# A two-block transformer layer on one core: the lo half of every fourth half unit of weights comes from an accumulating GpSimd DMA onto the negated hi half

## The chip, the cores and the metric

The kernel runs on one core of one Trainium2 chip. The core has a matrix engine (TensorE, PE in the profile; its weight loads are PEld), VectorE (DVE), ScalarE (ACT), GpSimd (POOL) and SyncE (SP), which issues most DMAs, and 16 DMA engines that all queues share. The metric is the device time of one execution in microseconds; lower is better.

## The reference

256 tokens of width 2048 pass through two blocks in fp32. Block 1 is differential attention beside retention, cross attention to a memory of 256 tokens, and a gated feed-forward; block 2 is spatial gating beside a gated linear recurrence, and a convolved feed-forward. Nearly all arithmetic lies in products of 256 rows with large weight matrices, for example:

```python
    h = rmsnorm(x, norm_mix_g[l])
    proj = h @ w_in[l]                     # 2048 x 6144
    ...
    x = x + mixed @ w_o[l]                 # 2048 x 2048
    ...
    x = x + (jax.nn.silu(hf @ w_gate[l]) * (hf @ w_up[l])) @ w_down[l]   # 2048 x 5632, 5632 x 2048
```

The results must hold to fp32-like accuracy.

## The kernel before

TensorE's fast format is fp32r, which keeps fewer bits than fp32. The kernel therefore splits each operand into two fp32r parts: `hi`, the value rounded, and `lo`, the value minus `hi`. A product is made of three matmuls, hi by hi, hi by lo and lo by hi.

The weights are a fixed list (`seq`) of 452 units of 1 MB, [128, 2048] fp32 each, in the order of their use. Every unit is used once. `fetch` loads a unit by one DMA on SP's queue into one of three raw buffers (tile `w`). `push` takes half a unit, 128x1024, and splits it: ScalarE casts it into `hi` (tile `wh`, line 129) and VectorE writes `lo` as the raw half minus `hi` (tile `wl`, line 130). `wh` and `wl` have five buffers each. The last five half units are split into other tiles, so 899 half units go through `wh` and `wl`.

`half` hands one half unit to a GEMM. Before it does, it pushes until five half units are in the list, so a half unit is split four half units ahead of its use. With five buffers, the buffers of half unit k are those of half unit k-5: the cast of half unit k starts when TensorE is done with half unit k-5, and is followed by the use of k-4, k-3, k-2 and k-1 before TensorE comes to k.

There are two kinds of GEMM. `gemm_fm` makes 256 output features by 256 tokens; a half unit is 8 matmuls with `wh` on 512 columns (line 297: the tokens' hi and lo side by side) and 8 with `wl` on 256 columns (line 301). Its first `wl` matmul is the second matmul of the half unit. There are 84 such GEMMs of four half units each. `gemm_tm` makes 256 tokens by 512 output features; a half unit is 12 matmuls on 512 columns (`mm3`, lines 145 to 147), and the first that reads `wl` (line 146) is again the second one.

Small work between the GEMMs (softmax, norms, convolutions, the scan) runs as generators that `tick` steps once per half unit. Each engine takes its instructions in its own order. GpSimd's queue holds 21 reciprocal square roots (`rsqrt`, line 151), 14 additions of squares (line 413) and two masks; it issues no DMA.

Of the kernel before, what the change touches and what calls it, by code (L numbers as in the profile page):

```python
# [8 lines left out]
F32 = mybir.dt.float32  # L9
F32R = mybir.dt.float32r  # L10
# [12 lines left out]
LOOKAHEAD = 4  # L23
TAIL = 5  # half units at the end whose operands stay for a second pass

# columns of the packed per-feature vectors
_COLS = [
# [17 lines left out]
def tile_kernel(ctx, tc, x, xT, mem, memT, par, alibi, rdecay, ident_d, bc_rows, gm_wsT,  # L45
# [29 lines left out]
    class Pair:  # L75
        """two k-tiles of a split operand: tiles of (hi | lo), or a tile of hi and one of lo"""

# [13 lines left out]
        def fill(self, src, gcols=None):  # L91
            """hi + lo == src * gain; src [P, 2, S] or two of [P, S]"""
            if gcols is None and not self.joined:
                split(self.t[0], self.t[1], src)
            else:
                for k in range(2):
                    split(self.hi(k), self.lo(k), src[:, k, :], None if gcols is None else gcols[k])
            return self
# [6 lines left out]

# [1 line left out]
    pr = cpool.tile([P, NPAR], F32, name="pr")  # L107
# [6 lines left out]
    V.memset(mhalf, -0.5)  # L114
    # the first activation table loads while the first data comes
    A.activation(st(1), mhalf[:, 0:1], AF.Square)
# [8 lines left out]

# [1 line left out]
    def split(hi, lo, src, gcol=None):  # L127
# [7 lines left out]
    def xpose_split(src, c, gcols=None, joined=False):  # L135
        """token-major src[t][:, c:c+256] -> split feature-major pair"""
        pt = sps().rearrange("p (k s) -> p k s", k=2)
        for k in range(2):
            for t in range(2):
                T.transpose(pt[:, k, t * P:(t + 1) * P], src[t][:, c + k * P:c + (k + 1) * P], ident)  # L140
        return Pair(joined).fill(pt, gcols)

    def mm3(out, lh, rh, start, stop):
        """both operands as (hi, lo)"""
        T.matmul(out, lhsT=lh[0], rhs=rh[0], start=start, stop=False)  # L145
        T.matmul(out, lhsT=lh[0], rhs=rh[1], start=False, stop=False)  # L146
        T.matmul(out, lhsT=lh[1], rhs=rh[0], start=False, stop=stop)  # L147
# [6 lines left out]
    class Sq:  # L154
        """sums of squares of token-major rows, piece by piece"""

# [18 lines left out]
    def rows(c):  # L175
        """[P tokens, 2] columns -> [P, 256], the same row in every partition"""
        d = flat(ft())[:, 0:S]
        for t in range(2):
            V.tensor_scalar(d[:, t * P:(t + 1) * P], ident, c[:, t:t + 1], None, ALU.mult)
        ps = sps()  # L180
        T.matmul(ps[:, 0:S], lhsT=ones, rhs=d, start=True, stop=True)
        r = spool.tile([P, S], F32, tag="rows", name=nm("rows"), bufs=3)
        A.copy(r, ps[:, 0:S])
        return r
# [3 lines left out]

# [1 line left out]
    seq = [(w_in_f, 0, u) for u in range(2)]  # L190
# [37 lines left out]
    def push():  # L228
        """one more half unit on its way"""
        w, g, u = seq[pos[1] // 2]  # L230
        h = pos[1] % 2
        if not raws:
            fetch()
        r = raws[0][:, 1024 * h:1024 * h + 1024]
        if h == 1:
            raws.pop(0)
        pos[1] += 1
        if pos[1] > 2 * len(seq) - TAIL:
            # kept until both halves of the tokens have used them
            hi, lo = [flat(rt()) for _ in range(2)], [flat(rt()) for _ in range(2)]  # L240
            for k in range(2):
                split(hi[k], lo[k], r[:, 512 * k:512 * k + 512])
        else:
            hi = whi.tile([P, 1024], F32R, tag="h", name=nm("wh"))
            lo = wlo.tile([P, 1024], F32R, tag="l", name=nm("wl"))
            split(hi, lo, r)
        feed.append((w, g, u, h, hi, lo))
# [10 lines left out]

# [1 line left out]
    bg = []  # L260
# [21 lines left out]
    def gemm_fm(wap, g, acts):  # L282
        """256 output features x 256 tokens: [P, m, (hi parts | lo parts)]"""
        ps = psg.tile([P, 2, 512], F32, tag="g", name=nm("pg"))
# [27 lines left out]
    def gemm_tm(wap, g, acts, k0=0, ps=None, tail=0):  # L312
        """256 tokens (2 banks) x 512 output features; in the last `tail` half units the second
        half of the tokens waits for the function that is returned"""
        if ps is None:
# [39 lines left out]
    def evac_split(ps, c):  # L355
        """token-major, as (hi, lo) for each half of the tokens"""
        res = []
        for t in range(2):
            hi, lo = flat(rt()), flat(rt())
            split(hi, lo, ps[t], need(c, 0)[:, t:t + 1])  # L360
            res.append((hi, lo))
        return res
# [10 lines left out]
    def operands(g, acts, gcols):  # L373
        """columns 512 g of the residual as operands of a GEMM"""
        for p in range(2):
# [4 lines left out]
    def next_in(g, acts, sq, gcols, after=None):  # L380
        """behind a residual update of columns 512 g"""
        if acts is not None:
# [8 lines left out]
    def stats(sq, rc, rr=None):  # L391
        """rstd of the rows as columns, and as a row in every partition"""
        rc[0] = sq.rstd(D)
# [4 lines left out]

    # =================================================================
    # block 1: projections, differential attention, retention  # L400
    # =================================================================
    def load(src, p):
# [4 lines left out]
    def load_split(f, gname, p, sq):  # L407
        a = Pair(True).fill(f, [col(gname, 2 * p + j) for j in range(2)])
        # sum of squares, feature-major
        s = ft()  # L410
# [7 lines left out]
    def col_stats(sq, n):  # L418
        """feature-major squares -> rstd as columns"""
        tot = sps()  # L420
# [10 lines left out]
    def x_gen():  # L431
        # loads (L), weight units (W) and splits (S) in the order in which they start
        n = 0
# [26 lines left out]

    # lambda = exp(q1.k1) - exp(q2.k2) + lam_init
    lam_init = 0.8 - 0.6 * math.exp(-0.3 * 0)
# [17 lines left out]
    def av_stage(pT, v, off):  # L480
        """[q, 256] = P^T.T @ v, causal in blocks of 128, and its sums of squares"""
        po = sps().rearrange("p (t e) -> p t e", t=2)
# [123 lines left out]

    # memory
    hm_a, sqm = [None] * 8, []
# [29 lines left out]

    # =================================================================
    # cross attention  # L640
    # =================================================================
    xk = []
# [6 lines left out]
    for g in range(4):  # L649
        if g == 3:  # L650
            # takes the space of the memory's operands, pair by pair
            spawn(chain([operands(i, hx_a, cols("norm_x_g", 0, 16)) for i in range(4)]))
# [50 lines left out]

    # =================================================================
    # feed-forward 1
    # =================================================================
    gg = cpool.tile([P, 16], F32, name="gg")
# [9 lines left out]
    def second_norm(g):  # L717
        # block 2 takes rmsnorm(x) * norm_f_g and normalises it again
        gf = flat(ft())
# [20 lines left out]

    # =================================================================
    # block 2: spatial gating and recurrent branch
    # =================================================================
    def tok(ins):
        # one order for the functions that share no activation table
        tc.stamp_issue_order_token(ins.ins, "tables")
        return ins
# [18 lines left out]

    # softplus(-lam) = max(-lam, 0) + log1p(exp(-|lam|))
    c8 = cpool.tile([P, 2, 8], F32, name="c8")
# [26 lines left out]
    def v_norm(t):  # L795
# [13 lines left out]
        for g in range(2):  # L809
            V.scalar_tensor_tensor(vg[t][g], vg[t][g], rr, gvg[g], ALU.mult, ALU.mult)  # L810
            V.tensor_tensor(vg[t][g], vg[t][g], gvb[g], ALU.add)
            yield
        # mixing over tokens, token-major
        for g in range(2):
# [10 lines left out]
    for f in ws:  # L825
        # keep s <= t
        f3 = f.rearrange("p (h t) -> p h t", t=P)
# [20 lines left out]

# [1 line left out]
    wa, wx = big(lru_wa), big(lru_wx)  # L850
# [29 lines left out]
    def lru_scan():  # L880
        for p in range(4):
# [5 lines left out]
            yield  # L887
            # 1 - exp(-2z) = tanh(z) * (1 + exp(-z)^2)
            d_ = ft()
# [84 lines left out]

    # =================================================================
    # feed-forward 2
    # =================================================================
    def conv3(z, c0):
# [36 lines left out]

    # last columns: the first half of the tokens leaves while the second is computed
    ps = [sps(), sps()]
# [98 lines left out]
```

## Time and profile before

| | |
|---|---|
| time, median of 2 runs | 2611.34 us (2611.17 to 2611.5) |
| span of the profiled execution | 2611.1 us |
| PE, PEld busy | 2590.6 us (99%), 2192.4 us (84%) |
| DVE, ACT, POOL busy | 1575.4 us (60%), 1292.5 us (50%), 38.1 us (1%) |
| HBM read | 486.39 MB, 187 GB/s over the span |
| granted TensorE clock | 0.999 of full speed |

The span runs from the first to the last instruction. The two timed runs lie 0.1 and 0.4 us above it, so next to nothing lies around the span. Matmuls overlap, so that a matmul of 390 ns is followed by the next after some 227 ns; the start times, not the durations, tell TensorE's pace.

### The profile page before, as it was taken

How to read it: one execution, taken by the hardware profiler on the slowest of the kernel's cores; microseconds unless marked ns; L12 is line 12 of the kernel's file. 1: busy time of each engine (PE TensorE's matmuls, PEld its weight loads, DVE VectorE, ACT ScalarE, POOL GpSimd, SP SyncE). 2: the span in 40 equal slices, each digit the busy share in tenths (PEclk: the TensorE clock that was granted, in tenths of full speed). 3: DMA queues.
4: the chain of work that ended last, by engine and by line, in shares of the span. 5: the costliest groups of instructions: out<-in, count | busy, mean ns of one | idle time of the engine just before them, and what ended most of it. 6: DMA issues, size and time to landing. Idle time of an engine off the chain costs nothing.

```text
span 2611.1 us, 32123 instructions
## 1 busy us (share of the span) xinstructions
PE 2590.6 (99%) x12922; PEld 2192.4 (84%) x12922; DVE 1575.4 (60%) x1889; ACT 1292.5 (50%) x1683; POOL 38.1 (1%) x41
## 2 busy tenths in 40 slices
PE   8999999999999999999999999999999999999998
PEld 7888888888888888888888888888888888888887
DVE  6665565556555454545454557866777745777754
ACT  5555554454454444334444555755555534555543
POOL 1000010000000000000000000000000000000000
PEclk9999999999999999999999999999999999999999
DMA  6455555554455555555555555554555555555563
GB/s 245 172 177 202 200 203 185 187 184 157 158 177 186 188 191 193 191 193 187 188 192 193 199 200 190 178 193 177 192 181 188 185 193 190 194 182 189 180 215 137
DMA packets 72726, 490.57 MB, mean 188 GB/s; under 512 B 8193, under 2 KB 8321, under 8 KB 14593
## 3 DMA queue, kind: packets, MB, share of 16 engines
q1 hardware_dynamic: 72576, 488.52, 53.2%
q8 instruction: 101, 1.65, 0.2%
q14 instruction: 49, 0.39, 0.0%
HBM read 486.39 MB, written 2.10 MB: 187 GB/s over the span
## 4 chain that ended last, share of the span: by engine, by line
PE 98%; issue 0%; DVE 0%; ACT 0%; DMA 0%; POOL 0%; SPq 0%; ACTq 0%; POOLq 0%; DVEq 0%
PE pg L297 24%; PE pg L145 19%; PE pg L146 19%; PE pg L147 19%; PE pg L301 12%; PE pp L140 1%; PE pp L147 1%; PE pp L146 1%; PE pp L145 1%; DMA w<-in_w_in_f_dram 0%; DVE r L133 0%; PE pp L818 0%; PE pp L871 0%; PE pp L870 0%; ACT junk L163 0%
## 5 line engine op out<-in xcount | busy, mean ns | idle before, releaser
L130 DVE TENSOR_TENSOR wl<-w,wh 128x1024 fp32r<-128x1024 f32 x899 | 1101.4, 1226 | 840.9 <-ACT wh L129 836.1
L129 ACT CAST wh<-w 128x1024 fp32r<-128x1024 f32 x899 | 944.1, 1051 | 983.2 <-PE pg L147 737.6
L297 PE MATMUL pg<-r,wh 128*128 128x512 f32 x2688 | 945.8, 401 | 12.0 <-ACT wh L129 7.3
L145 PE MATMUL pg<-wh,r 128*128 128x512 f32 x2224 | 870.2, 391 | 0.0
L147 PE MATMUL pg<-wh,r 128*128 128x512 f32 x2224 | 867.9, 390 | 0.0
L146 PE MATMUL pg<-wl,r 128*128 128x512 f32 x2224 | 867.5, 390 | 0.0
L301 PE MATMUL pg<-r,wl 128*128 128x256 f32 x2688 | 731.3, 283 | 0.5 <-DVE wl L130 0.5
L297 PEld LDWEIGHTS pg<-r,wh 128*128 128x128 f32 x2688 | 497.1, 189 | 120.0 <-ACT wh L129 7.3
L301 PEld LDWEIGHTS pg<-r,wl 128*128 128x128 f32 x2688 | 510.6, 190 | 17.6 <-DVE wl L130 1.0
L147 PEld LDWEIGHTS pg<-wh,r 128*128 128x128 f32 x2224 | 417.8, 188 | 86.4
L146 PEld LDWEIGHTS pg<-wl,r 128*128 128x128 f32 x2224 | 418.0, 188 | 85.6 <-DVE wl L130 0.4
L145 PEld LDWEIGHTS pg<-wh,r 128*128 128x128 f32 x2224 | 417.8, 188 | 84.4
L343 DVE TENSOR_TENSOR f<-pg,f 128x512 f32<-128x512 f32 x84 | 58.0, 691 | 90.2 <-ACT f L342 90.2
L342 ACT COPY f<-pg 128x512 f32<-128x512 f32 x84 | 49.2, 586 | 125.4 <-PE pg L297 125.4
L985 DVE SCALAR_TENSOR_TENSOR f<-f,pr,f 128x255 f32<-128x255 f32 x192 | 79.9, 478 | 0.7 <-ACT f L982 0.7
L982 ACT ACTIVATE f<-f,pr 128x256 f32<-128x256 f32 x96 | 52.6, 595 | 26.2 <-DVE f L344 26.1
L344 DVE TENSOR_TENSOR f<-f,rows 128x512 f32<-128x512 f32 x84 | 58.1, 691 | 2.6
L129 ACT CAST r<-f 128x512 fp32r<-128x512 f32 (+1 forms) x56 | 34.1, 610 | 16.3 <-DVE f L344 12.5
L371 DVE TENSOR_TENSOR xt<-xt,pg 128x512 f32<-128x512 f32 x54 | 34.7, 684 | 10.5 <-PE pg L147 10.5
L151 POOL TENSOR_TENSOR s<-s,mhalf 128x2 f32<-128x2 f32 (+1 forms) x21 | 14.3, 680 | 1783.0 <-DVE s L1026 802.7
L163 ACT ACTIVATE junk<-xt 128x512 f32<-128x512 f32 x48 | 30.2, 628 | 18.2 <-DVE xt L1022 17.2
L146 PE MATMUL pp<-r,r 128*128 128x256 f32 (+2 forms) x132 | 39.1, 299 | 0.0
(163 smaller groups left out, 860.8 us busy)
## 6 DMA issues: line engine op xcount, KB each, us to landing
w<-in_w_up_dram SPq DMA_DIRECT2D x140, 1024.0 KB, 4.8
w<-in_w_down_dram SPq DMA_DIRECT2D x92, 1024.0 KB, 4.8
w<-in_w_gate_dram SPq DMA_DIRECT2D x44, 1024.0 KB, 4.8
w<-in_w_in_t_dram SPq DMA_DIRECT2D x40, 1024.0 KB, 4.8
w<-in_w_in_f_dram SPq DMA_DIRECT2D x39, 1024.0 KB, 4.8
w<-in_w_o_dram SPq DMA_DIRECT2D x16, 1024.0 KB, 4.8
w<-in_w_xk_dram SPq DMA_DIRECT2D x16, 1024.0 KB, 4.8
w<-in_w_xv_dram SPq DMA_DIRECT2D x16, 1024.0 KB, 4.8
```

Of the source, the lines that this page charges most:

```text
L129: A.copy(hi, src)
L130: V.tensor_tensor(lo, src, hi.bitcast(F32), ALU.subtract)
L145: T.matmul(out, lhsT=lh[0], rhs=rh[0], start=start, stop=False)
L146: T.matmul(out, lhsT=lh[0], rhs=rh[1], start=False, stop=False)
L147: T.matmul(out, lhsT=lh[1], rhs=rh[0], start=False, stop=stop)
L297: T.matmul(ps[:, m, :], lhsT=hi[k][:, ms], rhs=a.both(k % 2), start=first, stop=last, skip_group_check=True)
L301: T.matmul(ps[:, m, S:], lhsT=lo[k][:, ms], rhs=a.hi(k % 2), start=False, stop=False, skip_group_check=True)
L342: A.copy(f, ps[:, :, S:])
L343: V.tensor_tensor(f, ps[:, :, 0:S], f, ALU.add)
L344: V.tensor_tensor(f, f, bc2(need(r, 0)), ALU.mult)
L982: A.activation(y[:, j, :], z[:, j, :], AF.Identity, scale=col("ffn_conv_w_2", 192 + c), bias=col("ffn_conv_b_2", c))
L985: V.scalar_tensor_tensor(y[:, j, d:], z[:, j, :S - d], col("ffn_conv_w_2", 96 * (2 - d) + c), y[:, j, d:], ALU.mult, ALU.add)
```

## The change

In `push`, every fourth half unit (the second half of every odd unit: k = 3, 7, 11, ... 895, 224 of the 899) makes its `lo` in another way. ScalarE casts the raw half into `hi` as before, then writes `-hi` into the `wl` buffer with a second instruction. Then GpSimd's queue issues a DMA that reads the same 512 KB of weights once more from HBM and adds them onto what lies in `wl`, which leaves the raw half minus `hi`. VectorE has no part in it. The other three of four half units, the buffers and the GEMMs stay as they are. The rest of the diff removes comments.

```diff
         else:
             hi = whi.tile([P, 1024], F32R, tag="h", name=nm("wh"))
-            lo = wlo.tile([P, 1024], F32R, tag="l", name=nm("wl"))
-            split(hi, lo, r)
+            if pos[1] % 4 == 0:
+
+                lo_ = wlo.tile([P, 1024], F32R, tag="l", name=nm("wl"))
+                A.copy(hi, r)
+                A.activation(lo_, hi.bitcast(F32), AF.Identity, scale=-1.0)
+                G.dma_start(out=lo_, in_=w[g, u][:, 1024 * h:1024 * h + 1024], accum_op=ALU.add)
+                lo = lo_
+            else:
+                lo = wlo.tile([P, 1024], F32R, tag="l", name=nm("wl"))
+                split(hi, lo, r)
         feed.append((w, g, u, h, hi, lo))
```

## Rows read from the trace of the kernel before

**Rows 1.** The page: the span, busy time of each engine, the granted clock in 40 slices, and the engines and lines of the chain that ended last.

```profile
span 2611.1 us, 32123 instructions
PE 2590.6 (99%) x12922; PEld 2192.4 (84%) x12922; DVE 1575.4 (60%) x1889; ACT 1292.5 (50%) x1683; POOL 38.1 (1%) x41
...
PEclk9999999999999999999999999999999999999999
...
PE 98%; issue 0%; DVE 0%; ACT 0%; DMA 0%; POOL 0%; SPq 0%; ACTq 0%; POOLq 0%; DVEq 0%
```

**Rows 2.** The waits of TensorE, all of them: who waited, for whom, us in total, times, longest.

```profile
PE pg L297 <- ACT wh L129: 7.3, 1, 7.3
PE pg L297 <- DVE r L133: 3.2, 4, 1.0
PE pg L297 <- DVE f L343: 1.5, 2, 0.7
PE pg L301 <- DVE wl L130: 0.5, 1, 0.5
```

**Rows 3.** The timeline of ScalarE, VectorE and TensorE around one fourth half unit (k = 739) in a `gemm_tm` of `w_down2`: start in us, us, engine, line, operation; in brackets the idle time before and what ended it. The cast at 2133.27 makes `wh` of k = 739; the line 145 matmul at 2133.07 begins half unit 735, that at 2143.95 begins half unit 739, and the one at 2144.18 is the first that reads its `wl`.

```profile
2133.27 1.05 ACT L129 CAST wh<-w 128x1024 fp32r<-128x1024 f32 x1 [1.67 <-PE pg L147]
2135.99 1.06 ACT L129 CAST wh<-w 128x1024 fp32r<-128x1024 f32 x1 [1.67 <-PE pg L147]
...
2134.36 1.23 DVE L130 TENSOR_TENSOR wl<-w,wh 128x1024 fp32r<-128x1024 f32 x1 [1.50 <-ACT wh L129]
...
2133.07 0.39 PE L145 MATMUL pg<-wh,r 128*128 128x512 f32 x1
...
2143.95 0.39 PE L145 MATMUL pg<-wh,r 128*128 128x512 f32 x1
2144.18 0.39 PE L146 MATMUL pg<-wl,r 128*128 128x512 f32 x1
```

**Rows 4.** The same around k = 635 in a `gemm_fm` of `w_up2`: its cast, and the second matmul of its use.

```profile
1841.62 1.05 ACT L129 CAST wh<-w 128x1024 fp32r<-128x1024 f32 x1 [1.77 <-PE pg L297]
...
1853.08 0.28 PE L301 MATMUL pg<-r,wl 128*128 128x256 f32 x1
```

**Rows 5.** The two fourth half units with the shortest time between cast and use, k = 107 in `w_o` and k = 571 in `w_in2_t`: the piece of ScalarE's timeline that holds the cast (at 331.60 two casts are merged, of which the first is k = 107, so it ends at some 332.6), and the first matmul that reads its `wl`.

```profile
331.60 1.98 ACT L129 CAST wh<-w 128x1024 fp32r<-128x1024 f32 x2
...
339.30 0.39 PE L146 MATMUL pg<-wl,r 128*128 128x512 f32 x1
...
1660.84 1.03 ACT L129 CAST wh<-w 128x1024 fp32r<-128x1024 f32 x1
...
1669.71 0.39 PE L146 MATMUL pg<-wl,r 128*128 128x512 f32 x1
```

**Rows 6.** Groups of instructions by line: busy us, mean ns of one, idle us before them and what ended it.

```profile
L130 DVE TENSOR_TENSOR wl<-w,wh 128x1024 fp32r<-128x1024 f32 x899 | 1101.4, 1226 | 840.9 <-ACT wh L129 836.1
L129 ACT CAST wh<-w 128x1024 fp32r<-128x1024 f32 x899 | 944.1, 1051 | 983.2 <-PE pg L147 737.6
L342 ACT COPY f<-pg 128x512 f32<-128x512 f32 x84 | 49.2, 586 | 125.4 <-PE pg L297 125.4
L129 ACT CAST r<-f 128x512 fp32r<-128x512 f32 (+1 forms) x56 | 34.1, 610 | 16.3 <-DVE f L344 12.5 <-DVE f L570 3.8
L411 ACT ACTIVATE f<-f 128x512 f32<-128x512 f32 x16 | 9.8, 616 | 0.0
L413 POOL TENSOR_TENSOR f<-f,f 128x512 f32<-128x512 f32 x14 | 21.6, 1543 | 72.2 <-ACT f L411 71.8
L828 POOL TENSOR_SCALAR_AFFINE_SELECT f<-f 128x512 f32<-128x512 f32 x2 | 2.0, 1024 | 712.1 <-DVE r L133 712.1
```

**Rows 7.** DMA: the queue of the loads (packets, MB, share of the 16 engines' span), issues (KB each, median us from issue to landing), and minimum, median and maximum of that time over all issues of tile `w`.

```profile
q1 hardware_dynamic: 72576, 488.52, 53.2%
...
w<-in_w_up_dram SPq DMA_DIRECT2D x140, 1024.0 KB, 4.8
f<-in_xT_dram SPq DMA_DIRECT2D x8, 256.0 KB, 7.8
out_dram<-xt SPq DMA_DIRECT2D x8, 256.0 KB, 2.4
...
DMA to landing us min/median/max: 4.4/4.8/8.9
```

**Rows 8.** The stretch from the start of half unit 735 to that of 739: its length, busy us of PE, PEld, DVE, ACT and POOL with instruction counts, granted clock, DMA share, GB/s.

```profile
2133.07:2143.95 10.88, 10.88 (x50) 9.02 (x48) 6.10 (x6) 4.22 (x4) 0.00 (x0) 1.00 0.57 194
```

**Rows 9.** Other waits: that of SP's queue before its weight loads, and the longest in sum that another engine spends on GpSimd.

```profile
SPq L224 <- DVE wl L130: 2310.9, 438, 10.4
...
ACT f L495 <- POOL s L151: 7.7, 6, 1.8
```

**Rows 10.** The chain that ended last, in order of time: the only two pieces on GpSimd among its 35 longest (start us, us, what).

```profile
123.86 0.70 POOL s L151
198.68 0.70 POOL s L151
```

## The prediction

> **What bounds the kernel now.** I read the page first. TensorE is busy 2590.6 of 2611.1 us, its clock is at the upper level (2.4 GHz) in every slice, and the chain that ended last lies on PE for 98% [rows 1]. That alone does not say whether TensorE ever waits for weights, so the second view is its waits: 7.3 + 3.2 + 1.5 + 0.5 = 12.5 us in all, of which the splitting of weights holds 7.3 + 0.5, once each [rows 2]. So TensorE runs through its list of matmuls, and VectorE (60%) and ScalarE (50%) follow it. Work taken off VectorE can return at most the waits that name VectorE, 3.2 + 1.5 + 0.5 = 5.2 us. Even all the time without PE, 20.5 us, is 0.8%. A measurement of this kernel tells some 2% (52 us) from no change, so nothing here can make it measurably faster. What is to be worked out is whether the new `lo` arrives in time.
>
> The third view is the timeline around one fourth half unit [rows 3]. Half unit 735 begins at 2133.07 and 739 at 2143.95: four half units take 10.88 us. The cast of 739 starts at 2133.27, when half unit 734 has let go of the buffer, and ends at 2134.32. TensorE first reads that `wl` at 2144.18. The **window** from the end of the cast to the first use is thus 9.86 us; I count with 9.85. The subtraction fills 2134.36 to 2135.59, so `lo` is ready 8.6 us early. In a `gemm_fm` the cast ends at 1842.67 and the use is at 1853.08, a window of 10.4 us [rows 4]. There is one fourth half unit to each four, so 84 of the 224 lie in the 84 `gemm_fm` (the x84 of L342) [rows 6] and 140 in `gemm_tm`. Two windows are short because ScalarE was late: 332.6 to 339.30, 6.7 us, and 1661.87 to 1669.71, 7.85 us [rows 5].
>
> **What the change removes.** 224 subtractions of 1.226 us [rows 6], 275 us of VectorE. It lies beside TensorE throughout and ends 8.6 us before its use, so it brings 0, at most the 5.2 us above. Who next waits for VectorE? SP's weight loads do, 2310.9 us in all [rows 9], but a raw buffer's load has three buffers' time and lands in 4.8 us [rows 7]; that wait is idling, not lateness. For odd units the buffer now comes free with the cast, 1.3 us sooner. That brings nothing either.
>
> **What it adds to ScalarE.** 224 writes of `-hi`, 128x1024 from SBUF. The nearest row is the cast of the same shape, 1.051 us [rows 6]. On 512 columns an ACTIVATE takes 616 ns (L411) and a cast 610 (L129 r<-f), so the form hardly matters [rows 6]. I take 1.06 plus 0.04 from one engine to the next (2134.32 to 2134.36) [rows 3]: 1.1 us. In all 235 us, hidden: in the stretch of four half units ScalarE works 4.2 of 10.88 us [rows 8] and would work 5.3. If that cover were gone, the next cast (2135.99 here, 1.67 us after the last) would start late by what the write exceeds the gap, and the cast itself has 9.85 us in hand.
>
> **What it adds to GpSimd's queue.** 224 DMA issues. The trace of before has no DMA from GpSimd. A GpSimd instruction of the program takes 0.7 to 1.5 us [rows 6, 10]; I take 1.0 for the issue, about the mask's 1.024, with 0.7 and 1.5 as bounds. Behind the issue, which waits for `-hi`, are queued the 14 additions and the 21 `rsqrt`. For `rsqrt` wait small ScalarE and VectorE steps, 7.7 us in all for the largest [rows 9]; two `rsqrt` stand on the chain [rows 10]. If each of these two is 1 us later, that is 2 us.
>
> **What it adds to the DMA engines.** The price of the whole case. The loads moved 488.52 MB in 53.2% of 2611.1 us [rows 7]: 2.84 us of all 16 engines per MB, or 2.98 us for a unit of 1.0486 MB. A unit lands 4.8 us after issue, so some 1.8 us of that are fixed. The added DMA reads 512 KB from HBM and must also read the 512 KB that lie in `wl`; its nearest row is one plain unit with as many bytes read, 3.0 us of engine time. Lower bound: a plain half unit, 1.5 us, or the 256 KB store's 2.4 us to landing. Upper bound from rows: the latest landing of any unit, 8.9 us, plus a GpSimd issue of 1.5, so 10.4.
>
> A rule of the Trainium skill bears on this price: its page "Collectives: The Full Stack" (The bandwidth ceiling) says that an add inside the DMA engines costs not by arithmetic but because it reads two sources, which halves the rate. By the plain price the landing would be 1.5 us sooner, by that rule it is mine; no run here shows an add.
>
> It competes with the plain loads: four half units need two, 2 x 2.98 = 5.96 of 10.88 us, 55%, as the stretch shows 57% [rows 8]. With 3.0 more it is 8.96 of 10.88, 82%: the engines still suffice. One load is issued when the cast ends, 1.1 us before the add, so they overlap; I add half a unit, 1.5 us. **Landing after issue:** 1.0 + 1.8 + 3.0 + 1.5 = 7.3 us. **From the end of the cast:** 1.1 + 7.3 = 8.4 us against windows of 9.85 and 10.4: in time by 1.45 us.
>
> A second rule speaks against the change: the Trainium skill's page "SBUF — State Buffer" (SBUF: two separate sides) warns that GpSimd cannot write a DMA's descriptors while VectorE runs an operation that uses both its ports. If every subtraction did that, an issue would lose up to 1.23 us and `lo` would come after 9.6 us, still in time. No row here shows a GpSimd DMA beside VectorE.
>
> **Sum.** Of the 224, two windows are too short: 8.4 - 6.7 + 8.4 - 7.85 = 2.3 us. With 2 us for the two `rsqrt`: 2611.1 + 2.3 + 2 = 2615.4, and I say 2616. The median of the runs stands 0.2 us over the span.
>
> **How a late landing would count.** With x us from the end of the cast to landing, a `gemm_tm` half unit is x - 9.85 late. That stall does not repeat each time: the window of half unit k+4 opens just as k comes up for use, so it grows by k's stall, and that landing is in time again. Late and timely alternate, which halves the price: loss = (140 (x - 9.85) + 84 (x - 10.4)) / 2, each bracket from zero up. It reaches 52 us (2%) at x = 10.52, a landing 9.4 us after issue. The row bound of 10.4 us gives x = 11.5 and 162 us.
>
> **The rivals.**
> *Late landing (slower).* The add takes half as much again on the engines, 4.5 us, say because a row's read and add do not overlap, and so meets more of the loads (2.5 us): 1.0 + 1.8 + 4.5 + 2.5 = 9.8, x = 10.9, loss 73.5 + 21 = 94 us: 2706. For it: my landing has only 1.45 us in hand, and units do land in up to 8.9 us. Against it: the engines are free 45% of the time, and half of what is late is returned. It decides from 9.4 us after issue.
> *Full DMA engines (slower).* If the add needs more than 10.88 - 5.96 = 4.92 us of the engines, the DMA engines set the pace. At 6.0 us, twice my price, four half units take 11.96 instead of 10.88: 2611 x 1.10 = 2870. For it: no row shows an add. Against it: that is four times the price of a plain half unit.
> *Relief of VectorE (faster).* All 20.5 us without PE would have to go: 2591, still within 2%. Faster by over 2% would need a faster TensorE, and nothing in the change touches its matmuls or its clock.
>
> **How the numbers follow.** In time: 0.57, at 2616, with its own range of 2606 (all 5.2 us come back) to 2640. Late landing: 0.28, from 2664 to some 2830. Full engines: 0.14, at 2870 or more. Faster: 0.01. The range of 2606 to 2840 leaves out the full engines, the end of the late landings and the faster case, some 0.18. Faster by over 2%: 0.01; within: 0.57; slower: 0.42.
>
> **What would show it.** Right: TensorE's waits name no `wl` DMA beyond a few us; the add's median landing is near 7.3 us and under 8.7; ACT has 224 more instructions of 1.05 us; DVE falls to some 1300 us, ACT rises to some 1530; the DMA share rises from 0.53 to some 0.79, or to 0.66 if the read from SBUF is not counted. Wrong: TensorE waits for `wl` at every second fourth half unit (late landing), or at all of them with the DMA share near its top in mid-kernel slices (full engines). A clock slice below 9 would mean stalls long enough to cost clock too, which my prices leave out.

## The result, and the profile after

The changed kernel takes 2624.83 us (median of 2 runs, 2624.02 to 2625.64), the kernel before 2611.34. The ratio is 1.0047, 95% interval [1.0031, 1.0064]: some 12 us slower (13.5 between these two medians), and within 2%. The profiled execution lasted 2625.64 us, with a span of 2623.9. The time stands 1.65 to 2.09 us above the span in every run that has both; the two timed runs of the kernel before, 0.1 and 0.4 us above its profiled span, were other executions than the profiled one, so a little more lies around the span than the section on time says. Span against span the change costs 12.8 us.

The page of the changed kernel, the lines that answer to [rows 1] and [rows 7]: span, busy time by engine, granted clock, and the two DMA queues (packets, MB, share of the 16 engines' span; q0 holds the adds).

```profile
span 2623.9 us, 32638 instructions
PE 2595.8 (99%) x12922; PEld 2192.5 (84%) x12922; DVE 1304.8 (50%) x1665; ACT 1524.9 (58%) x1907; POOL 231.4 (9%) x265
...
PEclk9999999999999999999999999999999999999999
...
q1 hardware_dynamic: 72576, 488.52, 54.4%
q0 software_dynamic: 32256, 117.45, 24.0%
```

Groups by line of the changed kernel, which answer to [rows 6], and the DMA issues (KB each, median us from issue to landing). The write of `-hi` is L249, the DMA issue L250.

```profile
L130 DVE TENSOR_TENSOR wl<-w,wh 128x1024 fp32r<-128x1024 f32 x675 | 826.0, 1225 | 770.9 <-ACT wh L129 765.9
...
L249 ACT ACTIVATE wl<-wh 128x1024 fp32r<-128x1024 f32 x224 | 237.3, 1060 | 6.2
...
L250 POOL DMA_DIRECT2D wl<-in_w_up_dram x70 | 60.7, 867 | 715.8 <-ACT wl L249 715.8
...
wl<-in_w_up_dram POOLq DMA_DIRECT2D x70, 512.0 KB, 6.4
```

275 us left VectorE, 232 us came to ScalarE, and the adds took 24.0% of the DMA engines: all as forecast. TensorE did the same 12922 matmuls in 5 us more of busy time. One add used 0.240 x 2623.9 / 224 = 2.81 us of all engines.

A typical fourth half unit, k = 739, the one of [rows 3]: timelines of ScalarE, GpSimd and TensorE (start us, us, what; in brackets the idle time before), the landing of its add (KB, us from the issue), and the stretch from its cast to the first matmul of k = 739, with the columns of [rows 8].

```profile
2144.28 1.05 ACT L248 CAST wh<-w 128x1024 fp32r<-128x1024 f32 x1 [1.67 <-PE pg L147]
2145.36 1.06 ACT L249 ACTIVATE wl<-wh 128x1024 fp32r<-128x1024 f32 x1
...
2146.72 0.86 POOL L250 DMA_DIRECT2D wl<-in_w_down_dram  x1 [10.02 <-ACT wl L249]
...
2155.18 0.39 PE L146 MATMUL pg<-wl,r 128*128 128x512 f32 x1
...
wl<-in_w_down_dram POOLq DMA_DIRECT2D x1, 512.0 KB, 7.5
```
```profile
2144.28:2154.96 10.68, 10.68 (x49) 8.82 (x47) 4.87 (x5) 5.28 (x5) 0.86 (x1) 1.00 0.82 242
```

The cast ends at 2145.33 and the first use is at 2155.18: the window is 9.85 us, as before. The issue starts 1.39 us after the cast. With the median landing of all 224 adds, 6.5 us, `lo` is ready 1.39 + 6.5 = 7.9 us after the cast, some 2 us before a use like this one; this add took 7.5 us and was 0.9 us early. TensorE runs through; ScalarE and the DMA engines (0.82 busy) keep up.

So the typical half unit costs nothing. Where do 12 us come from? The longest waits of TensorE behind one of 7.5 us at the start, which was 7.3 before (who waited, for whom, us in total, times, longest; the ten groups in all sum to 19.3 us, against 12.5 before [rows 2]):

```profile
PE pp L140 <- ACT f L503: 3.0, 2, 1.5
PE pg L146 <- DMA wl<-in_w_o_dram: 2.1, 1, 2.1
PE pg L305 <- DVE f L351: 1.5, 2, 0.7
PE pg L146 <- DMA wl<-in_w_down_dram: 1.3, 2, 1.0
...
PE pg L146 <- DMA wl<-in_w_up_dram: 0.7, 1, 0.7
```

Few and single: two waits on ScalarE's line 503, and five for an add (the fifth, 0.4 us, is for one of `w_in_f`). A new wait of 1.2 us on line 179 stands against 2.1 us less for `r` of line 133. The starts of the same half units in both traces (first matmul with `wh`) say where the kernel falls behind:

| half unit k | before, us | changed, us | behind, us |
|---|---|---|---|
| 8 | 40.76 | 41.25 | 0.5 |
| 36 | 126.76 | 128.68 | 1.9 |
| 66 | 219.79 | 224.31 | 4.5 |
| 104 | 330.92 | 335.65 | 4.7 |
| 112 | 353.63 | 362.61 | 9.0 |
| 516 | 1505.25 | 1515.70 | 10.5 |
| 898 | 2586.67 | 2598.92 | 12.3 |

Three parts: 4 us between k = 8 and 66, 4.3 us around k = 107 in `w_o`, 3.3 us spread over the other 790 half units.

**Around k = 107.** Timelines of ScalarE, GpSimd and TensorE of the changed kernel:

```profile
335.91 1.04 ACT L248 CAST wh<-w 128x1024 fp32r<-128x1024 f32 x1
337.75 0.91 ACT L132 ACTIVATE r<-f,pr 128x256 fp32r<-128x256 f32 x2 [0.80 <-DMA f<-in_memT_dram]
...
339.48 1.05 ACT L249 ACTIVATE wl<-wh 128x1024 fp32r<-128x1024 f32 x1
...
340.82 0.88 POOL L250 DMA_DIRECT2D wl<-in_w_o_dram  x1 [0.20 <-issue]
...
346.30 0.50 PE L146 MATMUL pg<-wl,r 128*128 128x512 f32 x1 [2.07 <-DMA wl<-in_w_o_dram]
```

The window was short, as [rows 5] had shown. The add itself was quick (it landed 5.4 us after its issue); but 2.5 us lie between the cast, over at 336.95, and `-hi`. In ScalarE's order small work of the memory tokens stands between the two, and ScalarE waited 0.80 us for its load (`memT`) before it did that work. These loads, eight of 256 KB from 300 to 345 us, took longer to land than before (median us, first the kernel before, then the changed one):

```profile
f<-in_memT_dram SPq DMA_DIRECT2D x8, 256.0 KB, 5.5
```
```profile
f<-in_memT_dram SPq DMA_DIRECT2D x8, 256.0 KB, 7.1
```

TensorE waited 2.07 us, and some matmuls later ran slowly for a while. The granted clock of two such stretches in the changed kernel, and last of the stretch of the same length in the kernel before (columns as in [rows 8]):

```profile
347.50:350.60 3.10, 3.10 (x8) 2.41 (x8) 2.52 (x3) 1.70 (x5) 1.65 (x1) 0.50 0.81 264
128.00:132.00 4.00, 3.32 (x11) 2.89 (x12) 3.28 (x7) 1.94 (x4) 0.00 (x0) 0.62 0.38 74
```
```profile
128.00:132.00 4.00, 4.00 (x24) 3.46 (x23) 3.93 (x7) 2.77 (x5) 0.00 (x0) 1.00 0.00 0
```

0.50 is the level of 1.2 GHz, 1.00 that of 2.4. The clock fell behind a wait of 2.07 us at 346 and behind two of 1.51 and 0.74 us at 127; the kernel before has only the second of these two there, 0.75 us, and kept its clock. At 0.50 over 3.1 us, 3.1 x 0.50 = 1.6 us are lost; at 0.62 over 4 us, 4 x 0.38 = 1.5 us. A page's digit of 9 hides both. Such a wait does not always cost the clock: the same two waits come again at 204 and 206 in this trace, and from 203 to 211 the clock was 1.00. The repeat below shows the like.

**The spread part.** The chain of work that ended last, in order of time (start us, us, what); of its 55 longest pieces those on an add behind k = 112, and the first of two casts (at 125 and 203 us) that the next section takes up:

```profile
125.56 1.05 ACT wh L129
...
1257.14 9.28 DMA wl<-in_w_up_dram
...
1503.20 9.81 DMA wl<-in_w_down_dram
...
1571.41 8.96 DMA wl<-in_w_in_f_dram
...
2494.24 9.54 DMA wl<-in_w_down_dram
```

Four adds landed after 9 to 9.8 us in place of 6.5. Three of them share the engines with small loads. SP's queue of the changed kernel just ahead of the last one, for which TensorE waited 0.95 us:

```profile
2489.92 2.05 SPq L1016 DMA_DIRECT2D f<-in_bc_rows_dram  x4
```

Four loads of 256 KB went out 2 to 4 us before the add. The like stands in SP's queue around 1503 (`gm_wsT`) and 1571 (`bc_rows`, `lru_wa`). The add at 1257 met slow loads of weights (7.0 to 8.2 us) only in this execution; in the repeat below it landed in 6.7 us.

**The part between k = 8 and 66.** The order of ScalarE around 125 us. First the kernel before, then the changed one with GpSimd and TensorE:

```profile
124.58 0.84 ACT L495 ACTIVATE f<-pp,s 128x256 f32<-128x256 f32 x2 [1.00 <-POOL s L151]
...
125.77 1.06 ACT L129 CAST wh<-w 128x1024 fp32r<-128x1024 f32 x1
```
```profile
124.24 0.87 POOL L250 DMA_DIRECT2D wl<-in_w_in_f_dram  x1 [10.39 <-ACT wl L249]
125.10 0.75 POOL L151 TENSOR_TENSOR s<-s,mhalf 128x2 f32<-128x2 f32 x1
...
125.56 1.04 ACT L129 CAST wh<-w 128x1024 fp32r<-128x1024 f32 x1 [0.75 <-PE pg L305]
126.51 0.83 ACT L503 ACTIVATE f<-pp,s 128x256 f32<-128x256 f32 x2
...
127.03 0.91 PE L140 MATMUL pp<-ident,f 128*128 128x128 f32 x4 [1.51 <-ACT f L503]
```

Two things differ. The reciprocal square root stands right behind a DMA issue on GpSimd. And ScalarE casts the next `wh` before it makes `f` (L503 is L495 of before); the chain names this cast. Which of them costs the 1.5 us, twice, is tried below.

### The profile page after: what moved, and what is told of

The parts are those of the page before. It is cut to its first block, busy times and chain, and to the rows that moved or that the text cites. A ratio compares the mean times of both kernels' runs of the same rounds, so it can differ in the third digit from the quotient of the medians.

```text
span 2623.9 us, 32638 instructions
## 1 busy us (share of the span) xinstructions
PE 2595.8 (99%) x12922; PEld 2192.5 (84%) x12922; DVE 1304.8 (50%) x1665; ACT 1524.9 (58%) x1907; POOL 231.4 (9%) x265
## 3 DMA queue, kind: packets, MB, share of 16 engines
q8 instruction: 101, 1.65, 0.2%
## 4 chain that ended last, share of the span: by engine, by line
PE 95%; DMA 3%; ACT 1%; issue 1%; DVE 0%; SPq 0%; POOL 0%; POOLq 0%; ACTq 0%
PE pg L305 23%; PE pg L146 19%; PE pg L147 19%; PE pg L145 19%; PE pg L309 12%; PE pp L140 1%; PE pp L147 1%; PE pp L146 1%; PE pp L145 1%; DMA wl<-in_w_down_dram 1%; DMA wl<-in_w_in_f_dram 1%; DMA wl<-in_w_up_dram 0%; DMA w<-in_w_in_f_dram 0%; DMA f<-in_memT_dram 0%; ACT wh L129 0%
## 5 line engine op out<-in xcount | busy, mean ns | idle before, releaser
L130 DVE TENSOR_TENSOR wl<-w,wh 128x1024 fp32r<-128x1024 f32 x675 | 826.0, 1225 | 770.9 <-ACT wh L129 765.9
L249 ACT ACTIVATE wl<-wh 128x1024 fp32r<-128x1024 f32 x224 | 237.3, 1060 | 6.2
L250 POOL DMA_DIRECT2D wl<-in_w_up_dram x70 | 60.7, 867 | 715.8 <-ACT wl L249 715.8
L250 POOL DMA_DIRECT2D wl<-in_w_down_dram x44 | 38.3, 870 | 438.2 <-ACT wl L249 405.1
```

The costliest lines, as they stand in the source:

```text
L130: V.tensor_tensor(lo, src, hi.bitcast(F32), ALU.subtract)
L249: A.activation(lo_, hi.bitcast(F32), AF.Identity, scale=-1.0)
L250: G.dma_start(out=lo_, in_=w[g, u][:, 1024 * h:1024 * h + 1024], accum_op=ALU.add)
```

## The experiments

First theory: the change is free for a typical half unit, and its 12 us are single events: adds that land after their window, and small work that comes late. Rival: the third stream costs a little everywhere, through contention or through the issues. Ratios are to the kernel before on the same chip, which ran 2612 to 2613 us there.

**The changed kernel again, five rounds.**

> The changed kernel, timed in five rounds beside the kernel before, as the base for the runs of the same call. Both theories: 2623 to 2626 us, 12 to 15 us over before. Theory 1 (single late arrivals): TensorE waits some 6 us more than before, in a handful of places, and its clock is at the lower level in two stretches more. Theory 2 (contention): each of the 224 added DMAs costs TensorE a little, 13 / 224 = 0.06 us.

Measured 2624.58 us, 1.005 [1.0036, 1.0065]. Its trace has the same two waits of 1.5 us and the same three `w_o` and `w_down` ones, 2.5 and 1.2 us. The loss belongs to the kernel, not to one execution. The clock's part is less fixed. Here it stayed at 1.00 behind the two waits at 127 us and behind the one of 2.54 us in `w_o` (346.7 to 350.7), and it fell behind the two at 203 and 205:

```profile
206.00:210.00 4.00, 4.00 (x18) 3.41 (x17) 2.71 (x5) 2.06 (x5) 0.00 (x0) 0.66 0.35 70
```

So waits of this length may cost the clock or not, and these traces don't show what decides it.

**No `lo` at all for every fourth half unit.**

```diff
             if pos[1] % 4 == 0:
-                lo_ = wlo.tile([P, 1024], F32R, tag="l", name=nm("wl"))
                 A.copy(hi, r)
-                A.activation(lo_, hi.bitcast(F32), AF.Identity, scale=-1.0)
-                G.dma_start(out=lo_, in_=w[g, u][:, 1024 * h:1024 * h + 1024], accum_op=ALU.add)
-                lo = lo_
+                lo = hi
```

> Leaves out the lo half of every fourth half unit (hi stands in its place), so neither VectorE's subtraction nor ScalarE's negation nor the DMA is there: the relief of VectorE alone. Theory 1 (TensorE is the bound, VectorE's relief returns at most its waits): 2606 to 2612 us, DVE at some 1300 us. Rival (VectorE's 1575 us hold something back): under 2600 us.

Measured 2610.26 us, 0.9991 [0.9982, 1.0]. VectorE is relieved by 270 us (1305.4 busy) and nothing replaces it: at most 0.2% comes back. The waits on ScalarE's small `f` are not there.

**The add beside the old split.** VectorE splits as before; the `-hi` and the add go into a spare tile that nothing reads. To make room, the pool of small tiles has two buffers fewer.

```diff
-    tpool = ctx.enter_context(tc.tile_pool(name="tpool", bufs=58))
+    wsp = ctx.enter_context(tc.tile_pool(name="wsp", bufs=1))
+    tpool = ctx.enter_context(tc.tile_pool(name="tpool", bufs=56))
...
-                lo_ = wlo.tile([P, 1024], F32R, tag="l", name=nm("wl"))
-                A.copy(hi, r)
-                A.activation(lo_, hi.bitcast(F32), AF.Identity, scale=-1.0)
-                G.dma_start(out=lo_, in_=w[g, u][:, 1024 * h:1024 * h + 1024], accum_op=ALU.add)
-                lo = lo_
+                lo = wlo.tile([P, 1024], F32R, tag="l", name=nm("wl"))
+                split(hi, lo, r)
+                sp = wsp.tile([P, 1024], F32R, tag="x", name=nm("ws"))
+                A.activation(sp, hi.bitcast(F32), AF.Identity, scale=-1.0)
+                G.dma_start(out=sp, in_=w[g, u][:, 1024 * h:1024 * h + 1024], accum_op=ALU.add)
```

> VectorE makes every lo as before, and the negation and the adding DMA run as well, into a spare tile that TensorE does not read (two buffers fewer for small tiles, to make room). Theory 1: without the wait for the DMA the late landings vanish, some 4 us of waits and one stretch at the lower clock, while the reciprocal square roots still stand behind DMA issues in GpSimd's queue: 2615 to 2621 us. Theory 2 (contention of the DMA, ScalarE's added 235 us): 2623 to 2626 us as the changed kernel, since all the added work is there.

Measured 2617.72 us, 1.0022 [1.0013, 1.0031]. All the added work is there, only TensorE doesn't wait for it. Against the changed kernel's 2624.58 some 7 us are gone: that is what waiting for adds costs, with the clock behind it. 5 us remain, and by the starts of its half units all of them are lost before k = 66 (4.9 us behind there, 4.95 at k = 898). There its trace has the two waits on ScalarE's line 503 as well. From k = 66 to the end 208 adds and 208 writes of `-hi` cost nothing, though a load now took 5.6 us to land and an add 8.0 (the wait on line 503, then load and add, us to landing):

```profile
PE pp L141 <- ACT f L503: 3.0, 2, 1.5
...
DMA to landing us min/median/max: 4.4/5.6/9.3
...
DMA to landing us min/median/max: 5.4/8.0/10.4
```

The rival has fallen for all but the first 66 half units.

**Only from k = 115 on** (`pos[1] % 4 == 0 and pos[1] > 112`), 196 adds.

> The change only from half unit 115 on: 196 of the 224 DMAs stay, the first 28 (the projections and half of w_o) go back to VectorE. Theory 1: in the changed kernel TensorE was 8.7 us behind by half unit 109 and lost only some 4 us in the remaining 790, so 2614 to 2617 us. Theory 2: 196 / 224 of 13 us stay, 2622 to 2624 us.

Measured 2617.07 us, 1.0016 [1.0007, 1.0025]: 28 of the 224 adds, the first, hold 7.5 of the 12 us. The two waits on L503 and that for `w_o` are not in its trace.

**Two half units given back to VectorE**, those whose issues stand ahead of the two reciprocal square roots.

```diff
-            if pos[1] % 4 == 0:
+            if pos[1] % 4 == 0 and pos[1] not in (40, 64):
```

> The changed kernel with two of the 224 half units, k = 39 and 63, given back to VectorE. Their DMA issues are the ones behind which the reciprocal square roots at 125.10 and 202.68 us stand in the changed kernel. First theory (of the 12 us some 5 come from TensorE waiting twice for these square roots and from the slower matmuls that follow): the two waits of 1.5 us that name ScalarE's line 503 go, and the time falls by 3 to 5 us, to 2619 to 2622. Rival (the loss lies in the DMAs themselves, spread over all 224): 222 of 224 of it stay, 2624.

Measured 2624.16 us, 1.0047 [1.0035, 1.006]: no gain, so the first theory missed here. Its timelines of GpSimd, ScalarE and TensorE; the last three lines are TensorE's first matmul of half unit 35, the last of the small products that `f` is made of, and the use of `f`:

```profile
124.76 0.71 POOL L151 TENSOR_TENSOR s<-s,mhalf 128x2 f32<-128x2 f32 x1 [11.23 <-DVE s L499]
...
125.24 1.04 ACT L129 CAST wh<-w 128x1024 fp32r<-128x1024 f32 x1 [0.78 <-PE pg L305]
126.19 0.83 ACT L503 ACTIVATE f<-pp,s 128x256 f32<-128x256 f32 x2
...
121.18 0.39 PE L305 MATMUL pg<-r,wh 128*128 128x512 f32 x1
...
123.17 0.28 PE L147 MATMUL pp<-r,r 128*128 128x256 f32 x1
...
126.72 0.91 PE L140 MATMUL pp<-ident,f 128*128 128x128 f32 x4 [1.51 <-ACT f L503]
```

The same two matmuls in the kernel before:

```profile
121.27 0.39 PE L297 MATMUL pg<-r,wh 128*128 128x512 f32 x1
...
122.22 0.28 PE L147 MATMUL pp<-r,r 128*128 128x256 f32 x1
```

The issue is gone from ahead of the square root, and TensorE waits the same 1.51 us. The square root is over at 125.47, and ScalarE doesn't make `f` before 126.19, because the cast stands ahead of it: 0.7 us. Counted from the start of half unit 35, `f` starts 5.01 us behind it here and 3.31 in the kernel before, 1.7 us later. The other 1.0 us of this is TensorE's own order: the last small product starts 1.99 us behind the start of half unit 35, and 0.95 in the kernel before. So it is the order of ScalarE and of TensorE, which is set when the kernel is built, and was built differently with the change. What in the change made the build choose it isn't settled. The two waits stand in the traces of the add beside the old split and of the plain copy (next), so they come neither from VectorE's relief nor from the addition; they are not in those of no `lo` at all and of five half units ahead (below).

**A plain copy in place of the add.** `lo` then holds the weights themselves; the bytes read from HBM are the same.

```diff
-                G.dma_start(out=lo_, in_=w[g, u][:, 1024 * h:1024 * h + 1024], accum_op=ALU.add)
+                G.dma_start(out=lo_, in_=w[g, u][:, 1024 * h:1024 * h + 1024])
```

> The same DMA without the addition: the weights land in lo and overwrite -hi, so lo is left out as a remainder. It prices the addition. Theory (the addition reads two sources): the queue's share falls from 24.3% to some 12%, the median landing from 6.6 to some 5.1 us; 2615 to 2621 us. Rival (the landing is mostly GpSimd's issue and fixed time): share near 24% or landing still over 6 us, 2623 to 2626 us.

Measured 2619.21 us, 1.0023 [1.0014, 1.0033]. The page, queue and issue:

```profile
q0 software_dynamic: 32256, 117.45, 13.5%
...
wl<-in_w_up_dram POOLq DMA_DIRECT2D x70, 512.0 KB, 5.2
```

A copy uses 0.135 x 2621.5 / 224 = 1.58 us of the engines, an add 2.81, and it lands 1.3 us sooner. The addition is what nearly doubles the price, and by the medians of the two kernels it is worth some 5 us of the time here.

**The issue later.** Four small additions on GpSimd, 0.83 us each and 3.3 us in all, ahead of each issue.

```diff
+                for _ in range(4):
+                    G.tensor_tensor(late, lo_[:, 0:256].bitcast(F32), lo_[:, 256:512].bitcast(F32), ALU.add)
                 G.dma_start(out=lo_, in_=w[g, u][:, 1024 * h:1024 * h + 1024], accum_op=ALU.add)
```

> The changed kernel with four small GpSimd additions (128x256, results unused) between the negation and the DMA issue, so that each landing is some 3 to 4.4 us later: 10.9 to 12.3 us after the cast instead of 7.9. By the prediction's formula (late and timely landings alternate) TensorE waits at about half of the 224 half units and loses 95 to 250 us: 2715 to 2870 us. Rival (each landing is late by itself): waits at nearly all 224 and twice the loss, 2810 to 3110 us. Second rival (there is more slack than the formula says): under 2650 us.

Measured 2704.79 us, 1.0355 [1.0324, 1.0386]: 80 us over the changed kernel, below the range. A part of the delay was returned: clear of the load ahead of it the add lands in 5.5 us, not 6.5. By the trace's records x, the time from the cast's end to the landing, has a median of 10.53 us, not the 7.9 + 3.3 = 11.2 that the delay alone would give. The formula of the prediction gives (140 x 0.68 + 84 x 0.13) / 2 = 53 us for that.

The profiled execution is the slowest of the four, 2717.08 us, 92 us over the changed kernel. Its waits for an add sum to 59.5 us, against 4.5 in the changed kernel; GpSimd's additions of squares, behind the four new ones, cost one wait of 6.2 us more; and the mean granted clock fell from 0.997 to 0.989, which is 0.008 x 2715 = 22 us: some 83 of the 92. The sum of the waits is near the formula, their number is not. TensorE waited 53 times, at a quarter of the 224 and not at half, for 1.1 us in the mean: the formula puts every half unit at the median x, and in the trace x varies, so fewer are late, and by more. That the sum fits is in part luck. Only 7 of the 53 were followed by a wait four half units on, where chance alone would give some 12: that a stall widens the next window is in line with it, but is not shown cleanly.

**Every second half unit** (`pos[1] % 2 == 0`), 449 adds.

> The change for every second half unit instead of every fourth, 449 DMAs. The changed kernel's added queue took 24.3% of 16 engines' span for 224 DMAs, 2.84 us each, against 2.98 us per plain unit. Theory 1 (full engines, the rival of the prediction at twice the load): four half units need 5.96 + 2 x 2.84 = 11.6 us of the DMA engines where TensorE needs 10.88: between 2690 and 2800 us, DMA share over 0.95. Rival (the engines' share is counted too high, because packets of two queues wait for each other): landing stays near 7 us and the time below 2650 us.

Measured 2740.2 us, 1.0471 [1.0428, 1.0513]. The page: DMA in 40 slices, and the queues.

```profile
DMA  9999999998899999999999999999999999999996
...
q1 hardware_dynamic: 72576, 488.52, 49.1%
q0 software_dynamic: 64656, 235.43, 47.1%
```

Here the engines are full: 96% of the span, 0.471 x 2743 / 449 = 2.88 us for one add. An add of `w_up` now landed 8.6 us after its issue, and TensorE's waits for an add sum to 85 us: full engines show as late landings. This is the rival of the full engines; at one in four they have a fifth of their time free.

**Three half units ahead,** the kernel before and the changed one (`LOOKAHEAD = 3`, `whi` and `wlo` with 4 buffers).

> The kernel before with one half unit less of lead (LOOKAHEAD 3, four buffers each of wh and wl), the control of the next run. VectorE's lo is ready 2.3 us after the cast begins, and the window shrinks from 9.85 to 7.1 us: 2611 to 2620 us by all theories.

> The changed kernel with LOOKAHEAD 3 and four buffers: windows of 7.1 us in gemm_tm and 7.6 in gemm_fm against a median of 7.9 us from cast to landing. The window of half unit k+4 now opens when k is done, so it holds no stall of k and nothing alternates: theory (a landing counts by what it exceeds its window): 140 x 0.8 + 84 x 0.3 = 137 us over the control, 2740 to 2780 us, TensorE waiting at most of the 224. Rival (stalls alternate here too): half of that, 2680 us. Rival (what counts is contention, not arrival): 13 us over the control.

Measured 2616.94 us, 1.0018 [1.0009, 1.0027], and 2745.71 us, 1.0517 [1.0477, 1.0557]. A window shorter by one half unit costs the kernel before 5 us and the changed one 121. This is the rival of the late landing: the same adds (6.5 us to landing in the middle), only less time. TensorE's waits name an add 69 times, 79 us in all; the time lay in the range, but waits at most of the 224 had been expected.

**Five half units ahead,** both again (`LOOKAHEAD = 5`, 6 buffers, the pool of small tiles cut from 58 to 54).

> The changed kernel with LOOKAHEAD 5 and six buffers each of wh and wl (four buffers fewer for small tiles, to make room): windows of 12.6 us. Theory (late arrivals): no wait of TensorE for a wl DMA is left after the first 30 us, the waits behind the reciprocal square roots stay: 2616 to 2621 us. Rival (contention): 2623 to 2626 us.

> The kernel before with half units split five ahead of their use in place of four (buffers 6, the pool of small tiles cut to 54): the control for the same edit on the changed kernel, which ran 2612.96 us. First theory (that edit repaid the changed kernel only by ending its late arrivals): nothing to repay here, 2610 to 2613. Rival (five ahead is faster by itself): 2605 or less, and the changed kernel would still be some 8 us behind it.

Measured 2612.96 us, 1.0005 [0.9996, 1.0015], for the changed kernel, and 2613.8 us, 1.0006 [0.9996, 1.0015], for the kernel before. With one half unit more in hand the change costs nothing and brings nothing, with its 224 adds in place. That is below both ranges that were stated for the changed kernel. The longer window is not all of it: there is no wait on line 503 in its trace either, since the build ordered that work anew, and a wait of 1.6 us for an add of `w_o` is left. No version beat the kernel before by more than its interval.

## Why the prediction was right, and where not

*TensorE bounds, and relief of VectorE brings nothing.* Right, and tried alone: 270 us less on VectorE returned some 2.6 us, hardly clear of noise and within the 5.2 us allowed.

*The window.* Right: 9.85 us in both traces.

*The path of the new `lo`.* Right, with two terms that err in opposite directions. From the cast to the issue I had 1.1 us and it is 1.39 (1.06 for `-hi`, as taken, and 0.30 from its end to the start of the issue, where I had 0.04). From issue to landing I had 7.3 and it is 6.5. Of this the issue is 0.87 (1.0 taken), the engines 2.81 (3.0 taken), and the overlap with the load 1.0 (1.5 taken): moved clear of the load the add landed in 5.5, and 0.87 + 1.8 + 2.81 is 5.5. So x is 7.9, not 8.4.

*The price of the addition.* I had taken the row of a whole unit, since an add must read both sources. The copy and the add, 1.58 against 2.81 us, show that the addition costs a factor of 1.8. The Trainium skill ("Collectives: The Full Stack", The bandwidth ceiling) says that two sources halve the rate; these runs show 1.8 where the rule has 2.

*No harm by VectorE at the issue.* By the records 42 of the 224 adds had VectorE busy for at least 0.9 of the 1.5 us from the start of their issue, and landed in 6.5 us in the middle; 164 with at most 0.6 us of VectorE's work beside them landed in 6.5 as well. An issue took 0.87 us. What did go with the landing is the time for which loads of weights ran beside it: 6.2 us in the middle with 3 to 4 us of them, 7.6 with over 5. So the warning of the Trainium skill ("SBUF — State Buffer", SBUF: two separate sides), that descriptors wait for VectorE's operations on both its ports, does not show here; these records don't sort VectorE's operations by the ports that they use.

*Two windows too short, 2.3 us.* Half right. The one in `w_o` cost 2.1 us of wait (1.7 forecast), but for a reason that was not in the sum: 2.5 us between cast and `-hi`, of which ScalarE waited 0.8 for a small load and spent 1.7 on small work. The step "what it adds to ScalarE" costed that write where ScalarE had a gap, and the prediction itself said that ScalarE was late there. The clock behind the wait took 1.6 us more, which the prices left out, as the prediction said. The other one landed 7.7 us after its cast with 7.85 in hand, and no wait names it.

*Two square roots behind an issue, 2 us.* The size was near, the step failed. Those two places did lose 1.5 us each, but not in GpSimd's queue: without the issue the wait stayed. The order, built anew, put a cast ahead of the small activation on ScalarE (0.7 us) and the small products further back on TensorE (1.0 us). The prediction took the order of all other work as given.

*In time by 1.45 us, so no other half unit waits.* Nearly. The median has 2 us in hand, but adds that meet other loads take 9 to 9.8 us and a few come late, 3.3 us in all. TensorE's waits for an add sum to 4.5 us, `w_o` included, in line with the few that were allowed. The prediction had one landing time for all 224.

*The sum.* 2616 was forecast, from a span of 2615.4; the profiled span is 2623.9. Of these 8.5 us some 3 are the clock behind two waits (the repeat has one such fall there), 3 the late adds beside other loads, 1 the waits on L503 beyond their term; the rest lies at the start (0.5 us) and the end (0.5) or is not sorted. From span to time 0.2 us were added, and it is 1.7.

*The rivals.* Each of the first two came true in a run that made its condition hold: late landing at three half units ahead or with a later issue, full engines with an add in every second half unit. The full engines' price was mis-sized: it set the engines against the 10.88 us of one stretch, but four half units take 2611 / 225 = 11.6 us in the mean, small work included. An add in every second half unit needs 2 x 2.88 + 5.96 = 11.7 us, just more than that. By the engines alone that is 1%; it cost 4.7%, mostly as waits for adds that landed late. The formula for late landings came near in the sum of the waits, not in their number, and left out the clock.

## What to carry to other kernels

Before work is moved to a DMA, compare the whole time from its source to its landing with the window of its use, place by place: here 7.9 against 9.85 us left the typical tile free, and the 12 us came from a few places: small work stood ahead of the write that the issue waits for, another load ran beside the add, or the build had ordered other work anew. One more tile in flight (and the order built with it) turned that into nothing, one less into 121 us; work taken off an engine that TensorE doesn't wait for returned under 3 us of 270. A change to one engine's work can also reorder a static schedule elsewhere, so compare the order of the engines in both traces before a wait is put down to what stands next to it.

## What the runs showed of the hardware

An accumulating DMA of 512 KB used 2.81 us of the 16 engines and a plain one on the same queue 1.58; the issue on GpSimd took 0.87 us for the add and 0.53 for the copy. TensorE's clock fell to its lower level for some 3 us soon after waits of only 1.5 to 2.1 us, and such a fall cost 1.5 to 1.6 us more; other waits of 1.5 us, and one of 2.54, left it at its upper level.
